# Cosine-similarity attention on one core: loads in pair order, and new orders on all engines

## The chip, the core and the metric

The kernel runs on one core of a Trainium2 chip. A core has five engines with a queue each, and each queue is worked off in the order in which the program wrote it: TensorE (PE: matmuls, and PEld, its weight loads), VectorE (DVE), ScalarE (ACT), GpSimd (POOL) and SyncE (SP, which here only issues DMAs). An instruction that waits for a semaphore holds everything behind it on its engine. The metric is the device time in microseconds; the median of the runs is compared.

## The reference

Attention on normalised vectors, for batch 8, 12 heads, 512 positions, dimension 64, in float32 (shapes are read from the inputs):

```python
Q_norm = Q / (np.linalg.norm(Q, axis=-1, keepdims=True) + 1e-10)
K_norm = K / (np.linalg.norm(K, axis=-1, keepdims=True) + 1e-10)
scores = np.einsum('bhqd,bhkd->bhqk', Q_norm, K_norm) / tau
weights = np.exp(scores - np.max(scores, axis=-1, keepdims=True))
weights = weights / (np.sum(weights, axis=-1, keepdims=True) + 1e-10)
return np.einsum('bhqk,bhkd->bhqd', weights, V)
```

With tau = 0.1 a score is at most 10 in size, so the kernel takes the exponential without subtracting the maximum.

## The kernel before

The 96 heads are worked as 48 pairs of heads, 0 to 47. Each step of a pair is one "operation" with a key, and the text names it by that key; s is the pair, w is 0 for Q and 1 for K, h the head in the pair, c one of four chunks of 128 keys.

- LD(s,w), LV(s): loads of Q, K and V of the pair, 256 KB each, issued by SyncE (lines 289 and 292; pair 0 in halves, line 286, K of pair 0 by ScalarE). ST(s): the store of the result (line 483).
- SQ(s): squares of Q and K together, on GpSimd (line 313, tile `sq`); for pairs 1 and 2 split over VectorE, ScalarE and GpSimd.
- RED(s,w): sums of the squares, on VectorE, either directly (line 341) or after TensorE has added part of them by SSQ(s,w) (lines 330 and 337).
- NEW(g,k): the reciprocal square root, for a group g of one or two pairs, in eight or nine small steps on VectorE (lines 362 to 371). For the first groups ScalarE does it instead: LOG(g), a logarithm, and NEW(g,7), an exponential (lines 355, 357; for pair 0 LOG and NRMS, lines 236, 240).
- SCL(s,w): Q or K times it (line 389): Q on VectorE, K on GpSimd for most pairs, on VectorE for ten of them.
- TR(s,w): transposes on TensorE (line 395); EVA(s): their copy out of PSUM on VectorE (line 402, tile `qt`).
- SCO(s,c): scores, two matmuls (line 429), into one of two halves of a score buffer; EXP(s,c): their exponential on ScalarE (line 445), 128x1024.
- VC(s): V to bf16 on GpSimd (line 450, tile `vb`). PV(s,h,i): weights times V on TensorE (line 459), with a column of ones that gives the sums. RCP and NRM(s,h): division on VectorE (lines 474, 476, tile `ob`).

`RINGS` sets how many buffers there are: 18 for Q and K, 6 for V, 6 for the squares, 3 each for the scaled and transposed values and the exponentials, 8 for the result. So LD(s) waits for SQ and SCL of pair s - 18, LV(s) for VC(s - 6), NRM(s) for ST(s - 8). While TensorE has nothing to do at the start, filler matmuls on zeros (`dummy`, line 188) stand in its queue.

The order of the operations on each engine is not worked out when the kernel is built. `schedule()` reads it from the constant `ORDER`: for each engine a list of numbers, each the place of an operation in the order in which the program adds it; a negative number is a filler of so many columns. `run()` then gives each operation its semaphore waits:

```python
order[e] = [self.list[int(x)] if x[0] != "-" else self.dummy(int(x[1:])) for x in text.split()]
```

Of the kernel before, what the change touches and what calls it, by code (L numbers as in the profile page):

```python
# [520 lines left out]
def slack(s, most):  # L521
# [5 lines left out]
        "7 8 64 65 103 104 143 142 224 223 11 180 181 257 105 66 258 144 182 377 334 299 300 376 333 225 259 378 453 "  # L527
        "410 487 562 335 563 301 452 411 529 715 605 412 486 528 222 987 944 945 681 639 179 564 63 606 716 791 682 454 "
        "640 102 530 141 488 911 868 758 757 607 1174 1064 1021 986 835 869 834 375 1098 332 256 836 717 451 792 298 "
        "409 641 910 683 1216 1063 1173 1139 759 793 1368 946 1402 1140 870 1020 561 638 527 912 680 1175 485 1097 1478 "  # L530
        "1444 1099 1141 988 1250 1479 604 1555 1326 1404 1215 1293 1522 1403 1249 1292 1521 1022 1065 1328 714 1674 790 "
        "1217 1369 1370 1251 867 756 1750 909 1445 985 1480 943 1749 1294 1556 1327 833 1631 1599 1632 1557 1783 1446 "
        "1825 1784 1708 1827 1709 1598 1096 1597 1062 1826 1138 1675 1673 1633 1172 1019 1523 1785 1751 1291 1214 1367 "
        "1707 1477 1248 1443 1325 1596 1401 1520 1748 1706 1630 1782 1554 1672 1824 1859 1860 "
    ),
    "pool": (
        "0 2 1 4 14 27 22 35 107 145 226 50 183 89 260 166 128 209 232 302 379 336 243 396 274 285 308 319 362 413 455 "
        "351 489 531 565 427 438 461 608 684 642 503 514 472 537 760 625 580 591 548 718 837 871 656 743 690 794 667 "
        "947 732 701 766 913 854 972 989 809 777 896 820 1066 930 1023 885 919 1201 1159 1100 1176 961 1430 995 1006 "
        "1125 1142 1218 1038 1083 1049 1354 1295 1371 1278 1114 1148 1235 1252 1507 1405 1190 1312 1388 1329 1224 1481 "  # L540
        "1267 1583 1617 1464 1447 1558 1846 1343 1524 1377 1600 1676 1419 1453 1693 1541 1811 1735 1634 1496 1769 1659 "
        "1752 1786 1710 1828 1572 1606 1648 1682 1724 1758 1800 1834 "
    ),
    "dve": (
        "5 13 15 26 28 19 67 24 21 32 70 72 37 34 75 109 78 111 76 80 114 117 149 147 115 227 119 152 155 153 184 186 "
        "229 61 187 62 188 55 189 190 56 191 157 192 263 100 194 193 101 195 196 198 94 230 95 200 303 261 305 139 133 "
        "264 140 265 134 266 234 267 380 268 171 269 271 172 270 177 339 272 337 382 178 276 340 306 341 214 342 220 "
        "343 221 344 310 345 215 346 347 254 349 255 414 348 248 416 249 385 456 353 383 458 290 417 291 418 296 419 "
        "297 420 421 490 422 387 424 423 492 324 425 325 330 532 566 429 459 367 534 368 493 331 494 609 495 463 496 "
        "373 497 374 498 401 568 499 500 685 402 407 501 408 643 505 535 611 443 569 444 570 449 571 572 450 573 574 "  # L550
        "539 575 576 612 578 477 483 645 478 577 484 582 761 614 687 519 646 520 647 525 648 526 649 719 650 616 721 "
        "651 553 653 652 554 559 654 688 560 838 658 763 596 722 597 723 602 724 603 725 795 726 727 692 729 728 636 "
        "872 630 730 797 631 637 764 734 840 672 798 673 799 948 800 678 801 914 802 768 803 679 805 804 874 807 706 "
        "806 707 712 841 990 713 811 916 748 875 749 876 843 877 878 754 879 755 880 882 881 845 883 782 783 788 950 "
        "789 1067 917 887 992 1024 951 825 952 953 826 831 954 955 956 958 957 832 921 1026 859 959 860 865 1177 866 "
        "1101 963 1069 901 1027 993 1028 907 1029 902 1030 908 1031 997 1032 1143 1033 1034 941 1036 935 1035 1103 936 "
        "1219 942 1070 1040 1145 1072 977 1104 1105 978 1106 1107 983 1108 984 1109 1296 1110 1111 1011 1179 1074 1012 "
        "1017 1112 1146 1372 1018 1116 1221 1180 1054 1181 1182 1183 1055 1184 1253 1060 1185 1061 1187 1186 1150 1188 "
        "1088 1222 1089 1094 1255 1095 1192 1406 1298 1130 1256 1131 1257 1258 1330 1259 1136 1260 1137 1261 1263 1262 "
        "1226 1265 1264 1482 1164 1332 1165 1170 1269 1171 1301 1374 1333 1206 1334 1299 1335 1212 1336 1207 1337 1338 "  # L560
        "1340 1213 1303 1339 1408 1240 1341 1246 1241 1247 1448 1375 1345 1450 1283 1409 1284 1410 1411 1289 1412 1290 "
        "1413 1414 1559 1416 1415 1417 1379 1317 1484 1323 1525 1318 1324 1451 1421 1527 1359 1485 1486 1487 1365 1488 "
        "1366 1489 1360 1490 1492 1491 1493 1455 1494 1399 1528 1393 1400 1394 1561 1601 1498 1530 1435 1603 1436 1562 "
        "1441 1563 1677 1564 1442 1565 1566 1635 1567 1532 1569 1568 1475 1711 1469 1470 1637 1476 1570 1512 1679 1513 "
        "1638 1574 1639 1640 1518 1641 1604 1642 1519 1643 1644 1645 1829 1608 1646 1552 1713 1546 1553 1547 1680 1650 "
        "1753 1755 1588 1714 1715 1716 1589 1717 1594 1718 1595 1719 1721 1720 1684 1722 1622 1789 1756 1623 1628 1726 "
        "1629 1787 1831 1664 1790 1791 1665 1792 1670 1793 1671 1794 1795 1796 1760 1832 1797 1704 1705 1698 1699 1798 "
        "1746 1747 1802 1740 1741 1836 1780 1774 1781 1775 1816 1817 1822 1823 1851 1852 1857 1858 "
    ),
    "pe": (  # L570
        "6 -256 -256 -256 20 23 -128 69 -256 -256 36 71 -128 42 33 38 108 39 43 110 46 79 77 48 148 81 146 83 118 116 "
        "85 51 52 57 58 87 53 54 59 120 185 60 228 122 154 156 124 96 97 98 99 126 262 90 158 91 92 160 135 93 136 137 "
        "162 138 197 199 164 129 130 131 132 201 304 233 203 205 231 173 174 207 167 168 169 175 170 235 176 338 237 "
        "210 211 212 213 239 381 275 273 241 216 217 218 219 277 309 279 307 281 250 251 252 253 283 244 245 246 247 "
        "311 350 415 292 313 293 315 286 287 294 352 317 288 295 289 457 354 386 384 356 320 321 322 358 323 491 360 "
        "326 327 328 329 388 390 426 428 392 363 364 365 366 394 533 430 462 460 432 397 398 399 369 400 434 370 371 "
        "372 436 567 464 403 404 405 406 466 439 440 468 441 502 504 470 442 445 610 506 446 447 448 508 538 536 510 "
        "473 474 475 479 476 512 644 480 481 540 482 542 579 581 544 515 516 517 521 546 518 686 522 523 583 524 615 "
        "585 613 549 550 551 587 552 720 555 589 556 557 558 617 619 592 593 594 655 621 595 657 762 623 598 599 600 "
        "601 659 689 661 626 627 632 628 691 663 633 634 635 665 629 796 693 695 731 733 668 697 669 670 671 839 699 "  # L580
        "674 675 676 735 767 677 765 737 702 703 704 739 705 873 741 708 709 710 769 711 808 771 744 745 746 747 810 "
        "773 915 775 750 751 752 842 812 753 814 844 778 779 816 780 784 781 785 818 949 786 787 846 884 848 821 822 "
        "823 886 824 850 991 827 828 852 920 829 888 830 918 890 855 856 857 858 892 1025 861 894 862 863 864 922 960 "
        "924 962 897 898 926 899 900 1068 928 903 904 905 906 996 964 994 966 931 932 937 938 968 933 939 940 934 970 "
        "1102 998 1037 1000 973 1039 974 975 1002 976 1144 979 980 1004 1041 1073 981 982 1043 1007 1008 1009 1045 1010 "
        "1178 1071 1047 1013 1014 1015 1016 1075 1077 1050 1115 1113 1079 1051 1052 1053 1220 1081 1147 1117 1056 1057 "
        "1149 1058 1059 1119 1084 1085 1086 1121 1087 1090 1091 1123 1092 1254 1151 1189 1093 1191 1153 1126 1127 1128 "
        "1155 1129 1297 1157 1132 1133 1223 1134 1193 1135 1195 1160 1161 1225 1197 1162 1166 1163 1199 1167 1331 1168 "
        "1169 1227 1268 1266 1229 1202 1203 1204 1205 1231 1373 1208 1233 1209 1302 1210 1211 1270 1272 1236 1237 1238 "
# [57 lines left out]
```

## Time and profile before

| | us |
|---|---|
| median of 6 runs | 193.68 |
| lowest and highest run | 191.94, 196.25 |
| the profiled execution, its time | 193.16 |
| the profiled execution, its span | 191.3 |
| ScalarE busy | 182.4 (95%) |
| TensorE, VectorE, GpSimd busy | 173.7, 168.3, 154.1 |
| first score exponential starts | 9.38 |
| last one ends | 187.98 |

Rows of the profile give, for groups of instructions, the line, the engine, what is written and read, the count, and after the bar the busy time and the mean length of one; then the idle time of the engine just before them and what ended it. In a timeline each row has start and length in us, and, in square brackets, the idle time of the engine before it and its releaser. A releaser is inferred; where it had long been done, another thing was waited for. Rows with "xN" merge N like instructions that follow each other. Consecutive instructions on one engine overlap a little in the records[...].

All of the 50.1 MB of loads and stores but 0.3 MB go through SyncE's queue (q1). The DMA engines are busy in nearly every slice up to 140 us, at 300 to 380 GB/s, and lightly after.

### The profile page before, as it was taken

How to read it: one execution, taken by the hardware profiler on the slowest of the kernel's cores; microseconds unless marked ns; L12 is line 12 of the kernel's file. 1: busy time of each engine (PE TensorE's matmuls, PEld its weight loads, DVE VectorE, ACT ScalarE, POOL GpSimd, SP SyncE). 2: the span in 40 equal slices, each digit the busy share in tenths (PEclk: the TensorE clock that was granted, in tenths of full speed). 3: DMA queues.
4: the chain of work that ended last, by engine and by line, in shares of the span. 5: the costliest groups of instructions: out<-in, count | busy, mean ns of one | idle time of the engine just before them, and what ended most of it. 6: DMA issues, size and time to landing. Idle time of an engine off the chain costs nothing.

```text
span 191.3 us, 6738 instructions
## 1 busy us (share of the span) xinstructions
PE 173.7 (91%) x2727; PEld 109.0 (57%) x2727; DVE 168.3 (88%) x588; ACT 182.4 (95%) x212; POOL 154.1 (81%) x143
## 2 busy tenths in 40 slices
PE   7799999988999898999999999999999989997973
PEld 2545655555666565656555656566655556564642
DVE  2689999989999889999999999999989989899533
ACT  4599999989999999999999999999999999999993
POOL 5399997999999799999999999999999984033000
PEclk9999999999999999999999999999999999999999
DMA  6999999999989999999999997799918033050083
GB/s 173 333 350 349 348 349 349 297 301 379 379 238 307 381 377 341 320 362 289 350 352 344 341 362 252 202 329 320 374 50 276 2 107 115 3 170 0 24 283 135
DMA packets 52302, 50.76 MB, mean 265 GB/s; under 512 B 3120, under 2 KB 52272, under 8 KB 52272
## 3 DMA queue, kind: packets, MB, share of 16 engines
q1 hardware_dynamic: 51984, 50.08, 80.4%
q8 instruction: 21, 0.34, 0.7%
q10 hardware_dynamic: 288, 0.26, 0.4%
q14 instruction: 9, 0.07, 0.1%
HBM read 37.75 MB, written 12.58 MB: 263 GB/s over the span
## 4 chain that ended last, share of the span: by engine, by line
ACT 58%; POOL 16%; DVE 8%; DMA 8%; SPq 3%; issue 3%; PE 2%; POOLq 0%
ACT et L445 58%; POOL sq L313 11%; DMA vf<-in_V_dram 4%; DMA qk<-in_Q_dram 3%; SPq L289 3%; POOL qn L389 2%; POOL vb L450 2%; DVE ob L476 2%; DVE qt L402 2%; DVE qn L389 2%; DVE nps L341 1%; PE ops L459 1%; PE scps L429 1%; PE tps L395 1%; DVE rd L474 1%
## 5 line engine op out<-in xcount | busy, mean ns | idle before, releaser
L445 ACT ACTIVATE et<-scps 128x1024 bf16<-128x1024 f32 (+1 forms) x195 | 177.4, 1105 | 1.0 <-PE scps L429 1.0
L313 POOL TENSOR_TENSOR sq<-qk 128x1024 bf16<-128x1024 f32 x45 | 84.7, 1898 | 2.0 <-DVE ob L476 1.2
L429 PE MATMUL scps<-qt 64*128 64x512 bf16 x384 | 75.5, 386 | 9.9 <-ACT et L445 6.4
L459 PE MATMUL ops<-vb,et 128*128 128x65 bf16 x1536 | 73.0, 194 | 0.4 <-DVE ob L476 0.3
L459 PEld LDWEIGHTS ops<-vb,et 128*128 128x128 bf16 x1536 | 56.0, 98 | 27.0 <-issue 17.0
L389 POOL TENSOR_TENSOR qn<-qk,rk 128x512 bf16<-128x512 f32 x37 | 38.5, 1048 | 14.2 <-DVE rk L367 8.9
L476 DVE TENSOR_TENSOR ob<-ops,rd 128x256 f32<-128x256 f32 x96 | 39.4, 415 | 1.0 <-DMA out_dram<-ob 0.6
L389 DVE TENSOR_TENSOR qn<-qk,nps 128x512 bf16<-128x512 f32 x57 | 37.9, 672 | 0.1
L395 PE MATMUL tps<-ident,qn 128*128 128x128 bf16 x376 | 33.9, 220 | 1.9 <-POOL qn L389 1.1
L429 PEld LDWEIGHTS scps<-qt 64*128 64x128 bf16 x384 | 19.0, 92 | 28.9 <-ACT et L445 12.7
L402 DVE COPY qt<-tps 128x1024 bf16<-128x1024 bf16 x47 | 32.1, 683 | 3.0 <-PE tps L395 2.8
L341 DVE TENSOR_REDUCE nps<-sq 128x8 f32<-128x512 bf16 x44 | 29.8, 682 | 1.5 <-POOL sq L313 1.5
L450 POOL TENSOR_SCALAR vb<-vf 128x512 bf16<-128x512 f32 x48 | 29.5, 632 | 1.5 <-DMA vf<-in_V_dram 1.0
L395 PEld LDWEIGHTS tps<-ident,qn 128*128 128x128 bf16 x376 | 21.6, 98 | 11.9 <-issue 3.2
L474 DVE RECIPROCAL rd<-ops 128x4 f32<-128x4 f32 x96 | 16.4, 173 | 7.1 <-PE ops L459 5.2
L330 PE MATMUL ops<-sq,ident 128*128 128x64 bf16 x400 | 20.0, 194 | 1.0 <-DVE sq L308 1.0
L330 PEld LDWEIGHTS ops<-sq,ident 128*128 128x128 bf16 x400 | 14.8, 98 | 7.0 <-issue 4.8
L337 DVE TENSOR_REDUCE nps<-ops 128x8 f32<-128x64 f32 x44 | 9.6, 220 | 1.8 <-PE ops L330 1.4
L363 DVE SCALAR_TENSOR_TENSOR nps<-nps,ys 128x32 f32<-128x32 f32 x44 | 8.5, 194 | 0.4
L362 DVE TENSOR_TENSOR nps<-nps,ys 128x32 f32<-128x32 f32 x44 | 8.4, 192 | 0.2
L367 DVE SCALAR_TENSOR_TENSOR nps<-nps,ys 128x16 f32<-128x16 f32 x29 | 5.0, 173 | 0.1
L185 PE MATMUL ops<-warm_in,ident 128*128 128x512 bf16 x8 | 3.6, 628 | 1.4 <-POOL ident L175 1.4
(43 smaller groups left out, 36.9 us busy)
## 6 DMA issues: line engine op xcount, KB each, us to landing
vf<-in_V_dram SPq DMA_DIRECT2D x48, 256.0 KB, 5.9
qk<-in_Q_dram SPq DMA_DIRECT2D x47, 256.0 KB, 6.3
qk<-in_K_dram SPq DMA_DIRECT2D x47, 256.0 KB, 5.8
out_dram<-ob SPq DMA_DIRECT2D x47, 256.0 KB, 4.7
qk<-in_Q_dram SPq DMA_DIRECT2D x2, 128.0 KB, 2.5
qk<-in_K_dram ACTq DMA_DIRECT2D x2, 128.0 KB, 2.7
out_dram<-ob SPq DMA_DIRECT2D x2, 128.0 KB, 1.7
```

Source lines behind the costliest of these rows:

```text
L313: lambda e: e.tensor_tensor(out=sqf, in0=data, in1=data, op=ALU.mult))
L330: last = e.matmul(out=o_ps[bank][:, 320:384], lhsT=ident[:, :], rhs=sq[iqs][:, 8 * w : 8 * w + 8, 8 * k : 8 * k + 8], start=(k == 0), stop ...
L341: lambda e, w=w, dst=dst: e.tensor_reduce(out=dst, in_=sq[iqs][:, 8 * w : 8 * w + 8, :], axis=AX.X, op=ALU.add))
L389: lambda e, w=w, r=r: e.tensor_tensor(out=qn[iqn][:, w].rearrange("p t h d -> p h t d"), in0=qk[iq][:, w].rearrange("p h (t d) -> p h t d" ...
L395: last = e.transpose(t_ps[:, w, t, :], qn[iqn][:, w, t].rearrange("p h d -> p (h d)"), ident[:, :])
L402: lambda e: e.tensor_copy(out=qt[iqt][:, :, :, :].rearrange("p w t x -> p (w t x)"), in_=t_ps[:, :, :, :].rearrange("p w t x -> p (w t x)")))
L429: last = e.matmul(out=sc_ps[:, 2 * b + h, :], lhsT=qt[iqt][64 * h : 64 * h + 64, 1, c, :], rhs=qt[iqt][64 * h : 64 * h + 64, 0, :, :], sta ...
L445: lambda e, c=c, b=b, hs=hs: e.activation(out=et[iet][:, c, hs[0] : hs[-1] + 1, :], in_=sc_ps[:, 2 * b + hs[0] : 2 * b + hs[-1] + 1, :], f ...
L450: lambda e: e.tensor_scalar(out=vb[:, iq, :, :, 0:DIM].rearrange("p c h d -> p h c d"), in0=vf[iv][:, :, :].rearrange("p h (c d) -> p h c ...
L459: last = e.matmul(out=o_ps[h][:, 65 * t : 65 * t + 65], lhsT=et[iet][:, c, h, 128 * t : 128 * t + 128], rhs=vb[:, iq, c, h, :], start=(c = ...
L474: lambda e, h=h, grid=grid: e.reciprocal(out=rd[io][:, h, :], in_=grid[:, :, DIM]))
L476: lambda e, h=h, grid=grid: e.tensor_tensor(out=ob[io][:, h], in0=grid[:, :, 0:DIM], in1=rd[io][:, h, :].unsqueeze(2).to_broadcast([128, N ...
```

## The change

Only the lists in `ORDER` change. The operations, their buffers and the waits of each on its data are the same; three fillers are added on TensorE. Written out in keys, the beginning of each list that moves (Q3 is LD(3,0), K3 is LD(3,1), V0 is LV(0)):

```
SyncE before   Q1 K1 Q2 K2 K3 Q3 K5 Q5 V0 Q4 K4 Q6 V2 V1 K6 V3 V4 K9 K8 Q7 K7 Q9 Q8 V5 V6 V9 K11 Q10
               K12 Q14 V8 K14 V7 ... ST2 V12 K23 Q22 K19 Q19 V15 K30 K27 K26 Q25 K21 K22 Q21 ST8 ...
SyncE after    Q1 K1 Q2 K2 V0 Q3 K3 V1 Q4 K4 V2 Q5 K5 V3 Q6 K6 V4 Q7 K7 V5 Q8 K8 V6 Q9 K9 V7 Q10 K10 V8
               Q11 K11 ST0 V9 ST1 V10 ST2 V11 ST3 ST4 Q12 K12 Q13 K13 Q14 K14 V12 Q15 K15 V13 Q16 K16 ST5
               V14 Q17 K17 ST6 V15 Q18 K18 ST7 V16 ... (one pair, one store, one V) ... Q47 K47 ST36 ...
GpSimd before  SQ2 SQ3 SQ5 VC0 SQ4 VC1 SQ6 VC3 VC2 VC4 SCL5 SQ7 SQ9 SQ8 VC5 VC9 SCL6 VC6 SCL7 VC7 VC8 SQ10
               SQ11 SCL8 SQ12 SQ13 SQ14 SCL10 VC10 SCL11 SQ15 SQ17 SQ16 SCL12 VC12 VC11 SCL13 SQ19 VC15
               SCL14 VC14 VC13 SQ18 SQ21 SQ22 SCL16 VC18 SCL17 SQ20 VC16 SQ24 SCL18 ...
GpSimd after   SQ2 VC0 SQ3 VC1 SQ4 SQ5 VC2 SQ6 VC4 VC3 SQ7 SCL5 SQ8 SQ9 VC5 SCL6 VC6 SCL7 VC7 SQ10 VC9 VC10
               SCL8 SQ11 VC8 VC11 SQ12 SQ13 SCL10 SCL11 SQ14 SQ15 SQ16 SCL12 VC14 VC12 SCL13 SQ17 SQ18 SCL14
               VC13 SQ19 SQ20 SQ21 SCL16 VC15 SCL17 VC16 SQ22 SQ23 VC17 SCL18 ...
ScalarE before LOG2 EXP(0,2) NEW(2,7) EXP(0,3) EXP(1,0) LOG3 EXP(1,1) NEW(3,7) EXP(1,2) ...
ScalarE after  LOG2 NEW(2,7) EXP(0,2) EXP(0,3) EXP(1,0) LOG3 NEW(3,7) EXP(1,1) EXP(1,2) ...
TensorE before warm, fillers 3x256, TR(0,0,0) TR(0,1,0), filler 128, SSQ(1,0), fillers 2x256, TR(0,1,1)
               SSQ(1,1), filler 128, SCO(0,1,0) ...
TensorE after  warm, fillers 5x256 192, TR(0,1,0) TR(0,0,0) SSQ(1,0), filler 192, TR(0,1,1), fillers 256 128,
               SSQ(1,1), filler 128, SCO(0,1,0) ...
VectorE before ... EVA1 NEW(2,6) SCL(2,1) RED(3,1) RED(3,0) SCL(2,0) RED(5,0) EVA2 ...
               ... NEW(6,3) NRM(4,1) NEW(6,4) EVA7 NEW(6,5) NRM(4,0) ...
VectorE after  ... NEW(2,6) EVA1 SCL(2,1) SCL(2,0) RED(3,0) RED(3,1) NEW(3,6) EVA2 ...
               ... NRM(4,0) NEW(6,2) RCP(4,1) NEW(6,3) NRM(4,1) NEW(6,4) EVA7 ...
```

In all of SyncE's new list Q, K of a pair come in the order of the pairs, and V and the stores in the order of theirs. On the other engines the lists differ in most places by a few positions: the scores keep their order on TensorE, the exponentials theirs on ScalarE. The diff, cut:

```diff
 ORDER = {
     "sp": (
-        "7 8 64 65 103 104 143 142 224 223 11 180 181 257 105 66 258 144 182 377 334 299 300 376 333 225 259 378 453 "
...
+        "7 8 64 65 103 104 11 142 143 66 180 181 105 223 224 144 257 258 182 299 300 225 333 334 259 376 377 301 410 "
...
     "pool": (
-        "0 2 1 4 14 27 22 35 107 145 226 50 183 89 260 166 128 209 232 302 379 336 243 396 274 285 308 319 362 413 455 "
...
+        "0 1 2 4 14 27 22 35 107 50 145 89 183 226 128 260 209 166 302 232 336 379 243 274 285 308 319 413 396 438 351 "
...
     "act": (
-        "9 10 3 12 25 16 17 18 29 30 31 68 106 73 44 74 40 41 45 112 47 113 49 82 150 84 151 86 88 121 123 125 127 159 "
+        "9 10 3 12 25 16 18 17 29 31 30 68 106 73 44 74 40 41 45 112 113 47 49 82 150 151 84 86 88 121 123 125 127 159 "
```

## The prediction

> **What bounds the kernel now.** I read the busy shares first, then ScalarE's timeline, then the chain back to what releases each late exponential, then GpSimd's and SyncE's timelines.
>
> ```profile
> PE 173.7 (91%) x2727; PEld 109.0 (57%) x2727; DVE 168.3 (88%) x588; ACT 182.4 (95%) x212; POOL 154.1 (81%) x143
> ```
>
> ScalarE is the bound: 182.4 of 191.3 us. Its timeline (start, duration) shows the rest:
>
> ```profile
> 4.51 0.30 ACT L236 ACTIVATE ys<-xs,eps 128x8 f32<-128x8 f32 x1 [0.22 <-DVE xs L233]
> 4.84 0.18 ACT L240 ACTIVATE scps<-ys 128x4 f32<-128x4 f32 x1
> ...
> 15.82 23.01 ACT L445 ACTIVATE et<-scps 128x1024 bf16<-128x1024 f32 x25
> 39.52 36.08 ACT L445 ACTIVATE et<-scps 128x1024 bf16<-128x1024 f32 x39 [0.70 <-PE scps L429]
> 75.87 112.11 ACT L445 ACTIVATE et<-scps 128x1024 bf16<-128x1024 f32 x123 [0.26 <-PE scps L429]
> ```
>
> After 9.38 us ScalarE stops visibly twice, at 39.52 (pair 7, chunk 3) and at 75.87 (pair 17, chunk 2). Consecutive exponentials overlap, so I count from end to end. The first one after a stop lasts 1.02 us in the same timeline, so the last row's first ends at 76.89, its second at 77.92 (the two take 2.05 us there), and the row at 187.98. From 77.92 on there are 119 full exponentials and two halves (0.49 us each): (187.98 - 77.92 - 0.98) / 119 = 0.917 us each. Against that pitch: 38.83 to 40.54 holds one exponential, 0.80 us lost; 40.54 to 75.60 holds 38, 0.21 lost; 75.60 to 76.89 holds one, 0.37 lost; 76.89 to 77.92 one, 0.11 lost. That is 1.5 us. Before 38.83 (24 in 21.99 us) and after 77.92 nothing is lost.
>
> GpSimd's and SyncE's timelines tell why:
>
> ```profile
> 32.53 1.22 POOL L450 TENSOR_SCALAR vb<-vf 128x512 bf16<-128x512 f32 x2 [0.98 <-DMA vf<-in_V_dram]
> 33.96 3.75 POOL L313 TENSOR_TENSOR sq<-qk 128x1024 bf16<-128x1024 f32 x2 [0.22 <-DMA qk<-in_K_dram]
> 37.66 1.04 POOL L389 TENSOR_TENSOR qn<-qk,rk 128x512 bf16<-128x512 f32 x1
> ...
> 63.29 3.75 POOL L313 TENSOR_TENSOR sq<-qk 128x1024 bf16<-128x1024 f32 x2 [1.20 <-DVE ob L476]
> ...
> 69.58 1.90 POOL L313 TENSOR_TENSOR sq<-qk 128x1024 bf16<-128x1024 f32 x1
> ```
> ```profile
> 49.16 0.62 SPq L292 DMA_DIRECT2D vf<-in_V_dram  x1
> 53.45 1.39 SPq L289 DMA_DIRECT2D qk<-in_K_dram  x3
> 54.88 0.47 SPq L289 DMA_DIRECT2D qk<-in_Q_dram  x1
> 55.41 0.97 SPq L289 DMA_DIRECT2D qk<-in_K_dram  x2
> 56.42 0.47 SPq L289 DMA_DIRECT2D qk<-in_Q_dram  x1
> ```
>
> First case: the 0.98 us is VC(7) waiting for V of pair 7, which SyncE issued at 23.91, behind V of pair 9, itself held for VC(3). GpSimd is full from there, so SCL(8,1) starts at 37.66; TensorE waits 0.85 us for it at the transposes of pair 8 (38.76), and the scores (7,3) stand behind those in its queue. Second case: the 1.20 us is SQ(21). Its releaser is named DVE, but that normalising multiply belongs to another pair; the load of Q of pair 21 is the 56.42 row. It was behind K of pair 30, for which SyncE stood still from 49.8 to 53.45, until pair 12 gave the buffer back. Hence SQ(20) ends at 71.5, VectorE waits 0.84 us for it in RED(20,0), SCL(18,0) comes at 73.96, TensorE waits 0.46 us at the transposes of pair 18 (74.67), and scores (17,2) are behind them. Both losses begin with a load that is issued out of its turn.
>
> **The change, part by part.** No instruction is added but three filler matmuls; the rest are moves. The sum starts from the profiled execution, 193.16 us (span 191.3, 1.86 outside it), 0.5 below the median 193.68.
>
> *Loads in pair order.* V(7) now stands behind the loads of pair 9 and waits only for VC(1); Q(21) stands behind ST(9), nine pairs ahead of K(30). Both waits above go, and with them the 1.5 us. A rule of the skill speaks against this: "SBUF — State Buffer", section "The DMA setup-cost knee", prices a transfer at about 2 us plus bytes over 436 GB/s, an estimate of 2.6 us for 256 KB. By it Q(21), issued at 56.42, lands at 59.0, before GpSimd asks at 62.1, and pair order gains nothing there. The trace's row is the one I use:
>
> ```profile
> qk<-in_Q_dram SPq DMA_DIRECT2D x47, 256.0 KB, 6.3
> ```
>
> With 6.3 us it lands at 62.7, near the 63.29 seen (longest Q or K load 8.7, shortest 2.4). The transfers are queued (about 349 GB/s from 5 to 33 us), so issue order is landing order.
>
> *GpSimd's order.* SQ(18) and SQ(20) move ahead by 4 and 7 us of work, SCL(8,1) ahead of SQ(11). From the rows, SQ takes 1.855 us, VC 0.585, SCL 1.01 (start to start). If SQ(3) starts at 11.5 (below), then 8 SQ + 9 VC + 3 SCL end and SCL(8,1) starts at 34.6, against 37.66 before. SQ(12) starts at 38.7 and SCL(12,1) at 50.0. On a clean clock chunk 0 of pair 12 is due at 38.72 + 17 x 0.917 = 54.3: lead 4.3. Before, SCL(12,1) started at 52.37 for a chunk due at 55.1, lead 2.75, and nothing was lost; so about 1.5 us of cover is left. VC steps come later in places (VC(36) by 36 us of work), but VC(36) at about 130 is for PV(36) near 145: nothing. What is late next is that same SCL(12,1), and SCL(22,1) with about as much lead.
>
> *Order of V(0).* It goes from eleventh to seventh on SyncE; Q(3) stays eighth, and K(3), which was seventh, becomes ninth. Q(3) landed at 10.72 and released GpSimd at 10.79; one more load at 349 GB/s is 0.75 us, so SQ(3) starts at about 11.5. VC(0) fills 0.6 of that. Cost by itself nothing, but ScalarE's LOG(3) hangs on SQ(3): SQ(3) ends at 13.4, its sums on TensorE at 14.0, and on VectorE RED(3,1) is now behind both SCL(2): copy of qt at 12.46, then 0.61 + 0.60 + 0.60 + 0.37, so 14.65. LOG(3) is reached at about 14.85. Cover 0.2 us; between 0 and, if K(3) takes the longest 8.7 us instead of 6.5, 2 us. I take 0.1, since the median load is near 6.5.
>
> *ScalarE's order.* The exponential that stood between LOG(2) and its own exponential, and the one behind LOG(3), move behind. The pair is now back to back and waits for its own semaphore. The head's rows show that form: 4.51 to 4.84, 0.33 us, while LOG(2) followed by a score exponential takes 0.20 (11.56 to 11.76). 0.12 us each, on the bound engine: +0.25. Two NRMS exponentials also swap, which gives VectorE its scale 0.12 us later; its copies stand behind SQ(1,0), which waits for Q(1) until 7.04: nothing.
>
> *TensorE and VectorE.* 640 more filler columns; two 256-column fillers take 0.21 us (8.04 to 8.25), so 0.27 us. 704 more go in front of the first transposes of pair 0, which feed copies that come at 7.65 anyway (cover about 0.5 us); 64 more stand between SSQ(1,0) and SSQ(1,1), 128 fewer in front. Uncovered it would be 0.27. Transposes sit on average a fraction of a chunk later before their scores, PV of head 1 later behind them; for pair 18 the lead falls from two chunks to one, as it was for pairs 4, 6 and 12 without loss. Bounds: -0.1 to +0.8 (the size of the largest loss seen); I take 0, because that lead of one chunk cost nothing where it was seen. The last PVs: four groups of head 1 now stand behind the last group of head 0, 16 x 0.04 us after data that ends 0.5 us earlier: 0 to 0.15, take 0.05.
>
> *Stores* wait in the same queue, ahead of loads. ST(4) is ahead of both loads of pair 12: rival 3.
>
> Sum: 193.16 - 1.5 + 0.25 + 0.1 + 0.05 = 192.06; I forecast 192.0.
>
> **Rivals.** *1, the wait only moves* (0.15). VectorE is 98% busy from 20 to 30 us and GpSimd without a gap; the 0.4 us by which GpSimd is behind at SQ(6), or RED(5,1) now after SQ(5) at 17.9 instead of 14.5, stops a transposition of pair 4 or 5, and the loss comes back: 193.2 to 193.7. For: TR(4) has one chunk of lead. Against: the two waits have named causes that go. *2, more than the seen loss goes* (0.17). The fastest of the runs before was 191.94, so the start-up varies by a few tenths; with LOG(3) in time and loads landing early, 191.66 less 0.3: 191.3. Against: nothing in the exponentials' pitch is left to win. *3, slower* (0.06): ST(4) holds LD(12). NRM(4,1) moves ahead of EVA(7), to about 33.3; K(12) is then issued at 34.2, and with landing time L SQ(12) starts at 34.2 + L. GpSimd is there at 38.7 with 1.5 us of cover, so the loss is L - 6.0. At the median 5.8 to 6.3 it is about nothing; over L = 7.7 the kernel is slower than its median; at 8.7 it is 194.8. For: every later load stands behind it. Against: by then 36 loads and four stores (10.5 MB) have gone through by about 33 us at 349 GB/s, so the queue is near empty and L nearer to 3.
>
> **How the numbers follow.** Likeliest case 0.62 at 192.0 (own range 191.6 to 192.6); rivals 0.17, 0.15, 0.06. Low end 191.3 from rival 2, high end 193.6 from rival 1; this leaves out rival 3 and the edges. A measurement of this kernel tells about 1% from no change: the runs before spread over 191.94 to 196.25. Faster by over 1% is below 191.74: rival 2 and a sixth of the likeliest case, 0.27. Slower by over 1% is above 195.6, the far end of rival 3 and what I have not thought of, 0.04.
>
> **What would show it.** In the profile after: ScalarE's row from 15.8 on unbroken, or broken by under 0.2 us; GpSimd without waits for loads between 12 and 150 us; SCL(8,1) near 34.6 and SQ(20) near 60; the LOG(2) to exponential distance 0.33; SQ(12) not waiting after ST(4). It is wrong if ScalarE shows a stop before 16 us (K(3)), or one near 40 to 55 us (K(12)), or if the median stays above 193 with an unbroken row, which would mean that the spread lies outside the stops.

## The result, and the profile after

The changed kernel takes 192.17 us (median of 28 runs, 191.27 to 193.00), the kernel before 193.55 us (median of 65 runs on the same chips, 191.94 to 199.38). The ratio is 0.9939, 95% interval 0.9921 to 0.9957: 0.6% faster, little, but clear of the noise. The medians of all runs are 1.4 us apart. The ratio leaves out the slow runs of the kernel before, those over 1.5% above its fastest; among the others the fastest are 0.7 us apart and the slowest 1.6 (194.56 against 193.00), so the change narrows the spread.

The page of the changed kernel's profile (granted clock in 40 slices; shares of the chain that ended last; DMA issues with the time to landing):

```profile
PEclk9889999999999999999999999999999999999999
...
ACT 91%; DMA 3%; PE 2%; DVE 1%; SPq 0%; ACTq 0%; issue 0%
...
qk<-in_Q_dram SPq DMA_DIRECT2D x47, 256.0 KB, 4.4
qk<-in_K_dram SPq DMA_DIRECT2D x47, 256.0 KB, 5.4
```

The loads of Q land 4.4 us after their issue (the median) where it was 6.3. The chain that ended last is now 91% ScalarE (58% before, with 16% GpSimd): once the exponentials run, nothing else is on it. ScalarE's timeline, the kernel changed:

```profile
10.39 0.31 ACT L355 ACTIVATE ys<-xs,eps 128x16 f32<-128x16 f32 x1 [0.83 <-DVE xs L337]
10.78 0.60 ACT L445 ACTIVATE et<-scps 128x512 bf16<-128x512 f32 x1
...
16.98 171.56 ACT L445 ACTIVATE et<-scps 128x1024 bf16<-128x1024 f32 x188
```

One row of 188 exponentials, from 16.98 to the last at 188.54: the stops at 39.5 and 75.9 are gone. Without the overlap of the first, (188.54 - 18.00 - 0.98) / 185 = 0.917 us each, the pitch of the kernel before without loss. The loss is nil.

This profiled execution took 193.87 us (span 191.8), 1.7 more than the median; it is not one of the 28. The excess lies ahead of the row: the first exponential starts at 10.78, not 9.38, and the granted clock is lower in slices 2 and 3 (more on this in the last section). A second profile of the changed kernel, experiment 8, has 191.60 us (span 189.6), the clock at 9 in every slice, the first exponential at 8.93 and the same row.

### The profile page after: what moved, and what is told of

Its sections match the earlier page's. It is cut to its first block, busy times and chain, and to the rows that moved or that the text cites. A ratio compares the mean times of both kernels' runs of the same rounds, so it can differ in the third digit from the quotient of the medians.

```text
span 191.8 us, 6749 instructions
## 1 busy us (share of the span) xinstructions
PE 176.8 (92%) x2730; PEld 111.2 (58%) x2730; DVE 169.0 (88%) x588; ACT 182.1 (95%) x212; POOL 154.5 (81%) x143
## 4 chain that ended last, share of the span: by engine, by line
ACT 91%; DMA 3%; PE 2%; DVE 1%; SPq 0%; ACTq 0%; issue 0%
ACT et L445 91%; DMA qk<-in_Q_dram 3%; PE ops L330 1%; PE scps L429 1%; DVE ob L476 0%; SPq L286 0%; DVE sq L308 0%; PE scps L188 0%; PE tps L254 0%; ACTq L85 0%; ACT xs L357 0%; PE scps L254 0%; ACT ys L355 0%; DVE rd L474 0%; PE ops L459 0%
## 5 line engine op out<-in xcount | busy, mean ns | idle before, releaser
L459 PE MATMUL ops<-vb,et 128*128 128x65 bf16 x1536 | 76.5, 194 | 0.2 <-ACT et L445 0.2
L459 PEld LDWEIGHTS ops<-vb,et 128*128 128x128 bf16 x1536 | 57.6, 98 | 29.6 <-issue 21.0
L429 PEld LDWEIGHTS scps<-qt 64*128 64x128 bf16 x384 | 19.6, 92 | 27.3 <-ACT et L445 10.3
L450 POOL TENSOR_SCALAR vb<-vf 128x512 bf16<-128x512 f32 x48 | 30.1, 637 | 1.9 <-DMA vf<-in_V_dram 1.4
L330 PEld LDWEIGHTS ops<-sq,ident 128*128 128x128 bf16 x400 | 15.3, 99 | 4.3 <-issue 2.2
```

Source lines behind the costliest of these rows:

```text
L330: last = e.matmul(out=o_ps[bank][:, 320:384], lhsT=ident[:, :], rhs=sq[iqs][:, 8 * w : 8 * w + 8, 8 * k : 8 * k + 8], start=(k == 0), stop ...
L429: last = e.matmul(out=sc_ps[:, 2 * b + h, :], lhsT=qt[iqt][64 * h : 64 * h + 64, 1, c, :], rhs=qt[iqt][64 * h : 64 * h + 64, 0, :, :], sta ...
L450: lambda e: e.tensor_scalar(out=vb[:, iq, :, :, 0:DIM].rearrange("p c h d -> p h c d"), in0=vf[iv][:, :, :].rearrange("p h (c d) -> p h c ...
L459: last = e.matmul(out=o_ps[h][:, 65 * t : 65 * t + 65], lhsT=et[iet][:, c, h, 128 * t : 128 * t + 128], rhs=vb[:, iq, c, h, :], start=(c = ...
```

## The experiments

Ranges in brackets are 95% intervals of the ratio to the kernel before, run on the same chip. "Lost" is what ScalarE's exponentials from (1,2) to (47,2) take over 0.917 us each, from end to end. Lists are written in keys, as in the section on the change.

### 1. SyncE's and GpSimd's new lists alone (e1_sp_pool)

```diff
-SyncE, GpSimd: lists of the kernel before
+SyncE, GpSimd: lists of the changed kernel
 VectorE, TensorE, ScalarE: lists of the kernel before
```

> The new lists of SyncE and GpSimd, the old ones of VectorE, TensorE and ScalarE. Theory A (the gain is the two late loads and GpSimd's place in the queue): the stops at 39.5 and 75.9 go, about 1.4 us off the kernel before, 0.2 more than the changed kernel's gain may be, since ScalarE's old order is kept: about 192.0. Rival B (the slack in VectorE's and TensorE's new lists carries the gain): at most a third of it, above 193.1, with stops left in ScalarE's row.

Measured: 210.99 us, ratio 1.0901 (1.0847 to 1.0955); lost 17.1 us. Every theory missed it. GpSimd's waits for the reciprocal root (in total, times, longest), and then one case on GpSimd and on VectorE:

```profile
POOL qn L389 <- DVE rk L367: 24.8, 11, 6.6
```
```profile
56.77 1.04 POOL L389 TENSOR_TENSOR qn<-qk,rk 128x512 bf16<-128x512 f32 x1 [3.10 <-DVE rk L367]
```
```profile
61.87 0.69 DVE L341 TENSOR_REDUCE nps<-sq 128x8 f32<-128x512 bf16 x1 [5.18 <-POOL sq L313]
```

GpSimd waits for VectorE's reciprocal root until 56.69. Two scalings and two V come next, and only then, at 59.95, the squares, for which VectorE has stood still since 56.69: each engine waits for the other in turn. So the lists go together, and a part of the gain can't be read off a part of the lists. If one follows the waits through all mixtures of whole old and new lists, only these run to the end: the kernel before, the new lists of SyncE and GpSimd together, and the new lists of SyncE, GpSimd, VectorE and TensorE together, each with either list of ScalarE. Every other mixture, SyncE's new list with GpSimd's old one among them, closes a circle of waits.

### 2. The changed kernel with ScalarE's old list (e2_act_before)

```diff
-ScalarE: LOG2 NEW(2,7) EXP(0,2) EXP(0,3) EXP(1,0) LOG3 NEW(3,7) EXP(1,1) ...
+ScalarE: LOG2 EXP(0,2) NEW(2,7) EXP(0,3) EXP(1,0) LOG3 EXP(1,1) NEW(3,7) ...
```

> The changed kernel with ScalarE's old list. Theory A: the two logarithms are followed by a score exponential again and take 0.20 instead of 0.33 us, so 0.25 us faster than the changed kernel (191.9). Rival: the distance costs nothing because the first scores come late anyway: the same 192.2.

Measured: 192.81 us, ratio 0.9976 (0.9952 to 1.0000): not the 0.25 us gain of an undone cost, rather a little slower than the change as a whole. Lost 0.72. VectorE's timeline and ScalarE's:

```profile
16.29 0.18 DVE L360 COPY nps<-xs 128x16 f32<-128x16 f32 x1 [1.39 <-ACT xs L357]
```
```profile
21.40 166.20 ACT L445 ACTIVATE et<-scps 128x1024 bf16<-128x1024 f32 x182 [0.58 <-PE scps L429]
```

In the new list of VectorE, NEW(3,6), the copy of what NEW(3,7) gives, stands ahead of EVA(2). An exponential between LOG(3) and NEW(3,7) makes VectorE wait 1.39 us there, EVA(2) with it, and five exponentials later ScalarE stops. The back-to-back order is the price of that place.

### 3 and 4. The two loads that the prediction named (e3_two_loads, e4_v7)

```diff
 SyncE of the kernel before (4: the first line alone)
-... V5 V6 V9 K11 ... Q8 V7 ...        V15 K30 K27 K26 Q25 K21 K22 Q21 ...
+... V5 V6 V7 V9 K11 ...               (unchanged in 4)
+                                      V15 Q21 K30 K27 K26 Q25 K21 K22 ...
```

> The kernel before with two loads moved and nothing else: V of pair 7 ahead of V of pair 9, Q of pair 21 ahead of K of pair 30. Theory A: GpSimd's waits at 32.5 (0.98) and 63.3 (1.20) go, ScalarE's row is whole from 15.8 on, 192.0 to 192.2. Rival B: the next late thing takes over at once, 193.2 or more. Rival C (the gain is not two named loads but the spread of landing times over all loads): the profile is whole in one execution, yet the median falls by less than half, 193.

> The kernel before with only V of pair 7 moved ahead of V of pair 9. Theory A: the stop at 39.5 (0.80 and what follows, 1.0 us) goes, the one at 75.9 (0.48) stays or grows, because GpSimd waits longer for Q of pair 21: 192.6 to 192.9. Rival B: no change, 193.5.

Measured: both loads 193.11 us, ratio 0.9975 (0.9947 to 1.0003); V(7) alone 193.59 us, 1.0008 (0.9978 to 1.0037). GpSimd's and ScalarE's timelines with both moved:

```profile
33.18 3.74 POOL L313 TENSOR_TENSOR sq<-qk 128x1024 bf16<-128x1024 f32 x2 [0.90 <-PE scps L429]
36.88 1.04 POOL L389 TENSOR_TENSOR qn<-qk,rk 128x512 bf16<-128x512 f32 x1
```
```profile
38.74 148.11 ACT L445 ACTIVATE et<-scps 128x1024 bf16<-128x1024 f32 x162 [0.52 <-PE scps L429]
```

The wait for V(7) is gone, and GpSimd waits 0.90 us at SQ(10) instead, whose K load is late next (the row names TensorE, but K(10) landed at 33.11 and SQ(10) starts at 33.18). SCL(8,1) still stands behind SQ(10) and SQ(11), starts at 36.88, and the stop at 39 stays: 0.74 lost there. In 4, V(7) alone moved (profiled execution 195.06 us, 3.6 lost), it is the same: SCL(8,1) at 37.33, a stop of 0.59 us at 39.19. So the stop of pair 7 doesn't hang on V(7) alone. The stop at 75.9 shows in neither 3 nor 4, though in 4 Q(21) was not moved. At most part of the gain is in these two loads.

### 5. SyncE's list of the kernel before, remade by need (e5_need_order)

```diff
 all other lists: kernel before
-SyncE: ... V6 V9 K11 Q10 K12 Q14 V8 K14 V7 Q11 K10 K13 Q18 Q15 V10 Q12 Q13 ST4 K25 ...
+SyncE: ... V6 Q10 V7 K10 Q11 K11 V9 V8 ST0 Q12 K12 Q13 ST1 K13 Q14 K14 ST2 V10 Q15 K15 ...
```

> The kernel before with SyncE's list alone made anew: each load in the turn in which GpSimd's old list asks for it, as soon as its buffer is free; all other lists old. Theory A2 (the order of all loads carries the gain, the two named ones were only this execution's): GpSimd hardly waits for loads, the slow executions go, median 192.0 to 192.5 with highest under 194. Rival D (the new lists of GpSimd, VectorE and TensorE carry it, by slack): 193.0 or more, with the stop near 39 still there, as SCL(8,1) stands behind SQ(11).

Measured: 200.87 us, ratio 1.0371 (1.0317 to 1.0424), lost 9.7. No theory had that. One line of GpSimd's timeline:

```profile
96.84 0.63 POOL L450 TENSOR_SCALAR vb<-vf 128x512 bf16<-128x512 f32 x1 [4.79 <-DMA vf<-in_V_dram]
```

GpSimd waits 10.5 us in four places for V. They are V of pairs 9, 24, 29 and 32. In this list V stands behind stores, and SyncE stands still for 58 us at stores and 12 at V (summed from the gaps of its timeline), with everything behind them. But the changed kernel's SyncE stands still for 73 us at stores and loses nothing, so the standing by itself is not the cost; what is lost depends on which loads stand behind, and that isn't worked out here.

### 6. The changed kernel, LOG and NEW apart, VectorE arranged for it (e6_act_dve)

```diff
 ScalarE: list of the kernel before
-VectorE: ... NEW(2,6) EVA1 SCL(2,1) ...  NEW(3,6) EVA2 ...
+VectorE: ... EVA1 NEW(2,6) SCL(2,1) ...  EVA2 NEW(3,6) ...
```

> The changed kernel with ScalarE's old list, and on VectorE the copies EVA(1) and EVA(2) ahead of NEW(2,6) and NEW(3,6), as they were. If the loss with ScalarE's old list alone came from VectorE waiting for NEW(2,7) and NEW(3,7) with the copies behind, it goes here, and the 0.25 us that the back-to-back exponentials cost come off: 191.9. Rival (the first 16 us are set by landings, so neither matters): 192.2 to 192.4, like the changed kernel.

Measured: 191.94 us, ratio 0.9896 (0.9865 to 0.9927); the changed kernel on the same chip 191.63 us, 0.9890 (0.9826 to 0.9954). No gain (the changed kernel has four runs there). From the first score exponential to the end of EXP(1,2) ScalarE takes 7.47 us in the kernel before, 7.74 in the changed one (experiment 8) and 7.86 here. So the price of back-to-back, 0.27 us, is there, and undoing it exposes another wait: LOG(3) starts at 14.21, when the sums of SQ(3) are ready, and waits for them.

### 7. The changed kernel, each V from pair 6 on two pairs later (e7_v_late2)

```diff
-SyncE: ... Q8 K8 V6 Q9 K9 V7 Q10 K10 V8 Q11 K11 ST0 V9 ST1 V10 ST2 V11 ST3 ST4 Q12 K12 Q13 K13 Q14 K14 V12 ...
+SyncE: ... Q8 K8 Q9 K9 Q10 K10 V6 Q11 K11 ST0 V7 ST1 V8 ST2 V9 ST3 ST4 Q12 K12 Q13 K13 Q14 K14 V10 ...
```

> The changed kernel with each V from pair 6 on issued two pairs later (in the place of V two pairs on). Theory A2: GpSimd waits for V again, ScalarE's row breaks in several places from 40 us on: 193 to 196. Rival D: the slack of the new lists takes it up, 192.2 to 192.5.

Measured: 241.56 us, ratio 1.2436 (1.2306 to 1.2566), lost 48.6: slower, as the theory of V's place had it, but by far more. SyncE's timeline, then GpSimd's:

```profile
31.76 2.48 SPq L483 DMA_DIRECT2D out_dram<-ob  x2
34.28 0.47 SPq L289 DMA_DIRECT2D qk<-in_Q_dram  x1
...
37.38 0.47 SPq L292 DMA_DIRECT2D vf<-in_V_dram  x1
```
```profile
42.73 0.63 POOL L450 TENSOR_SCALAR vb<-vf 128x512 bf16<-128x512 f32 x1 [8.73 <-DMA vf<-in_V_dram]
```

V(10) is the row at 37.38: behind ST(3), ST(4), which wait for their pairs until 34.2, and behind six loads of Q and K. It lands 5.3 us later, GpSimd has stood at VC(10) for 8.73 us, and SCL(8,1) behind it. ScalarE's next exponential waits 8.35 us, so ST(5) is issued at 49.60 only, and the V behind it still later. It feeds on itself: 51 us of waits for V in 13 places.

### 8. The changed kernel again (e8_changed_again)

> The changed kernel once more, for a second profile: if the late first exponential of its profiled execution (10.78 against 9.38 us) belongs to that execution, it is near 9.4 here and the span near 190.3; if it belongs to the new filler list, it is above 10 again with the granted clock of TensorE below 0.9 in the first 10 us. ScalarE's row whole from 16 us on in both cases; median 192.2.

Measured: 191.63 us (four runs, 191.60 to 191.64), ratio 0.9890 (0.9826 to 0.9954). ScalarE's timeline:

```profile
8.93 0.58 ACT L445 ACTIVATE et<-scps 128x512 bf16<-128x512 f32 x1
...
11.11 0.31 ACT L355 ACTIVATE ys<-xs,eps 128x16 f32<-128x16 f32 x1
11.45 0.22 ACT L357 ACTIVATE xs<-ys 128x16 f32<-128x16 f32 x1
...
14.75 171.56 ACT L445 ACTIVATE et<-scps 128x1024 bf16<-128x1024 f32 x188
```

GpSimd's:

```profile
35.07 1.04 POOL L389 TENSOR_TENSOR qn<-qk,rk 128x512 bf16<-128x512 f32 x1 [0.41 <-DVE nps L367]
...
39.10 3.74 POOL L313 TENSOR_TENSOR sq<-qk 128x1024 bf16<-128x1024 f32 x2
...
92.46 1.89 POOL L313 TENSOR_TENSOR sq<-qk 128x1024 bf16<-128x1024 f32 x1 [0.50 <-DMA qk<-in_K_dram]
...
127.34 1.89 POOL L313 TENSOR_TENSOR sq<-qk 128x1024 bf16<-128x1024 f32 x1 [0.86 <-DMA qk<-in_K_dram]
```

And SyncE's, at K(12), behind ST(3), ST(4) and Q(12):

```profile
34.87 0.49 SPq L289 DMA_DIRECT2D qk<-in_K_dram  x1
```

ScalarE's row is whole, and yet GpSimd waits 4.5 us for loads from 12 us on, against 3.0 in the profile before (the 1.2 at SQ(21), whose releaser is named VectorE, included). But the waits lie elsewhere. Between 24 and 125 us, where all stops of the first profile before are, GpSimd waits 2.3 to 4.4 us for loads in the kernel before and its load orders (before, 3, 4, 10, 12; the longest wait 0.9 to 1.4; counted by the landings, since the names are inferred). In the five profiles with the new lists on SyncE, GpSimd, VectorE and TensorE (after, 2, 6, 8, 11) it waits 0.3 to 0.8 us, 0.5 the longest; V(7) and Q(21) are in time in all five. Their waits after 125 us are longer, 3.7 us here. So in the stretch where loads were late before, they are now in time.

### 9. As 5, with the stores later (e9_need_stores_late)

```diff
-SyncE (5): ... Q11 K11 V9 V8 ST0 Q12 K12 Q13 ST1 K13 Q14 K14 ST2 V10 Q15 K15 ...
+SyncE (9): ... Q11 K11 Q12 V9 V8 K12 Q13 K13 Q14 K14 V10 Q15 K15 ST0 Q17 K17 Q16 K16 V12 ST1 ...
```

> As the list by need, but each store put where its pair has been divided for some 8 us in the profiled execution of before, so that SyncE should not stand at a store with loads behind it. All other lists old. Theory S (a V load behind a store that SyncE stands at is what costs; the order of loads by itself is worth the 1.4 us): 192.0 to 192.6. Rival D (the gain needs the new lists of GpSimd, VectorE and TensorE): 193.0 to 194.0, with SyncE and GpSimd hardly waiting for one another, and ScalarE's stop near 39 still there.

Measured: 199.68 us, ratio 1.0324 (1.0264 to 1.0385), lost 8.35. It decides nothing. GpSimd waits 8.8 us for V in four places (longest 4.0), SyncE stands 23 us at V for a buffer and 44 at stores. Fewer waits at stores, more at V: which of the two holds the loads isn't told apart.

### 10. The kernel before again (e10_before_again)

> The kernel before, for a second profile. Theory C (its stops move from one execution to the next with the landings): ScalarE's row breaks again near 39, and at other places than 75.9, with GpSimd waiting for other loads than V of pair 7 and Q of pair 21. Rival: the same two stops at the same places, 0.9 and 0.5 us.

Measured: 197.90 and 195.52 us, slower than 43 and 40 of the 43 other runs of the kernel before on this chip (191.40 to 196.60). The profiled execution (197.90) on ScalarE, then on GpSimd:

```profile
58.34 45.02 ACT L445 ACTIVATE et<-scps 128x1024 bf16<-128x1024 f32 x49 [0.76 <-PE scps L429]
103.90 5.61 ACT L445 ACTIVATE et<-scps 128x1024 bf16<-128x1024 f32 x6 [0.54 <-PE scps L429]
110.02 82.81 ACT L445 ACTIVATE et<-scps 128x1024 bf16<-128x1024 f32 x91 [0.52 <-PE scps L429]
```
```profile
101.45 0.62 POOL L450 TENSOR_SCALAR vb<-vf 128x512 bf16<-128x512 f32 x1 [1.27 <-DMA vf<-in_V_dram]
```

The same program stops at 57, 58, 104 and 110 us, and neither at 39 nor at 76. Lost 2.7 us against 1.5 in the first profile. But it is not a second sample of the same conditions. The clock is low at its start (last section), and EXP(1,2) ends 3.6 us later than in the first profile, while V(7) lands at 31.74, earlier than the 32.45 there: GpSimd asks for it at 35.08 only, so it is in time, and the stop of pair 7 is gone. That stop is there in the three profiles that start in time, with SCL(8,1) behind both squares and the stores where they were (before, 3, 4). The stops at 104 and 110, pair 24 chunk 0 and pair 25 chunk 2, come again in 4 and in 12. So the places are not drawn anew each time: the kernel before has a few weak places, and which of them open depends on the execution. That this also holds between two executions that both start in time is not shown.

### 11. Experiment 6 with the sums of SQ(3) earlier (e11_first16)

```diff
-SyncE: ... K2 V0 Q3 K3 V1 Q4 ...       GpSimd: SQ2 VC0 SQ3 VC1 ...   VectorE: ... SCL(2,0) RED(3,0) RED(3,1) EVA2 ...
+SyncE: ... K2 Q3 K3 V0 V1 Q4 ...       GpSimd: SQ2 SQ3 VC0 VC1 ...   VectorE: ... RED(3,0) RED(3,1) SCL(2,0) EVA2 ...
```

> The changed kernel with ScalarE's old list, EVA(1) and EVA(2) ahead of NEW(2,6) and NEW(3,6), and further V of pair 0 behind K of pair 3 on SyncE, SQ(3) ahead of VC(0) on GpSimd, RED(3,0) and RED(3,1) ahead of SCL(2,0) on VectorE. If LOG(3) waits for SQ(3), and that ate what ScalarE's old list gives back, SQ(3) starts 0.7 us earlier and 0.25 to 0.4 us come off the changed kernel: ratio to before 0.985 to 0.992 where the changed kernel has 0.989 to 0.994. Rival (something else holds the first scores): no difference from the changed kernel.

Measured: 192.07 us, ratio 0.9938 (0.9914 to 0.9961): no better than the changed kernel. LOG(3) no longer waits, but GpSimd does at 18.79 (1.22 us, for a load), and ScalarE stops at 20.33 (0.23) and 21.51 (0.16). The wait has moved by some five microseconds. No version tried beats the changed kernel clearly.

### 12. The kernel before, both seen stops taken away at their roots (e12_loads_scl8)

```diff
-SyncE: ... V5 V6 V9 K11 Q10 K12 ... V7 Q11 K10 ...   Q21 ahead of K30, as in 3     GpSimd: ... SQ10 SQ11 SCL8 ...
+SyncE: ... V5 V6 V7 Q10 K10 V9 K11 K12 ...                                          GpSimd: ... SQ10 SCL8 SQ11 ...
```

> The kernel before with five moves: V of pair 7, Q and K of pair 10 ahead of V of pair 9, Q of pair 21 ahead of K of pair 30, and SCL(8,1) ahead of SQ(11) on GpSimd. My first theory, completed (the two seen stops are the loss): no stop at 39 or 76, 192.0. Rival C (most of the loss of the median lies in stops that change from run to run): the profile is nearly whole, yet the median is 192.9 or more, and the highest runs stay above 195.

Measured: 193.72 us, ratio 1.0000 (0.9965 to 1.0036). ScalarE's timeline:

```profile
60.00 38.79 ACT L445 ACTIVATE et<-scps 128x1024 bf16<-128x1024 f32 x42 [0.16 <-PE scps L429]
99.27 5.61 ACT L445 ACTIVATE et<-scps 128x1024 bf16<-128x1024 f32 x6 [0.47 <-PE scps L429]
105.39 83.67 ACT L445 ACTIVATE et<-scps 128x1024 bf16<-128x1024 f32 x91 [0.52 <-PE scps L429]
```

The stops at 39 and 76 are gone, as wanted, and the kernel loses 3.1 us, at 60, 99, 105 and in smaller pieces. Nothing gained in 22 runs. The stops at 99 and 105 have one root. SyncE's, GpSimd's and TensorE's timelines:

```profile
89.97 0.43 SPq L292 DMA_DIRECT2D vf<-in_V_dram  x1
```
```profile
96.82 0.62 POOL L450 TENSOR_SCALAR vb<-vf 128x512 bf16<-128x512 f32 x1 [1.35 <-DMA vf<-in_V_dram]
97.41 1.04 POOL L389 TENSOR_TENSOR qn<-qk,rk 128x512 bf16<-128x512 f32 x1
```
```profile
98.51 0.40 PE L395 MATMUL tps<-ident,qn 128*128 128x128 bf16 x4 [0.51 <-POOL qn L389]
```

Counted off in the lists, the V is that of pair 36, and the scaling behind it is SCL(25,1). V(36) needs the buffer of V(30), which VC(30) gives back at 89.94, and it takes 6.8 us to land. GpSimd's old list asks for it 5.5 us after VC(30), just ahead of SCL(25,1): TensorE waits 0.51 us for it at the transposes of pair 25, and the scores (24,0) stand behind those. GpSimd has no gap from there to SCL(26,1), which is then late for (25,2). It is the same V(36) at 101.45 in 10. In the first profile before, V(36) landed 5.2 us after its issue, and GpSimd waited 0.05 us. So the root is GpSimd's order: it takes a V eleven pairs ahead of its turn and stands at it. In the new list VC(36) comes in its turn, at 131.80 in experiment 8, 9.9 us after V(36) has landed.

## Why the prediction was right, and where it was not

The time was right, 192.0 for 192.17, and so was the likeliest case, faster by less than 1%. The reason given for the largest term was wrong in part. The number did not suffer, since it needs only that the loss goes, and not what caused it.

**The floor: right.** It was 193.16 less 1.5 lost. The rows of both profiles of the changed kernel have nothing lost, at the same 0.917 us. What was to be won was the loss and no more; rival 2's 191.3 is the fastest run (191.27), not the median. That the profile before was of a middling execution, 0.5 us below its median, was luck: the same sum from the execution of 10, 197.90 us with 2.7 lost, would have given 195.6.

**Loads in pair order: the size right, the cause right only in part.** "Both waits above go" held: V(7) and Q(21) are in time in all five profiles with the new lists. The step that failed is "Both losses begin with a load that is issued out of its turn", and with it "and with them the 1.5 us". Moving the two loads gave 0.9975, one of them 1.0008, and taking both stops away at their roots 1.0000.

What the runs show in its place: the losses begin on GpSimd as much as on SyncE. The stop of pair 7 stays with V(7) in time, since K(10) is late in its stead and SCL(8,1) stands behind both squares (3, 4). It goes when SCL(8,1) moves ahead of a square and V(7), Q(10) and K(10) come earlier, all together (12). The stops of pairs 24 and 25 (4, 10, 12) begin with V(36), which GpSimd takes too early. The prediction looked at that move, "VC(36) by 36 us of work", asked only what it costs, and put it at nothing; that the old place could cost something was not considered. In the old list GpSimd takes V up to 15 pairs ahead of the last pair whose K it has scaled, in the new one up to 5.

"GpSimd without waits for loads between 12 and 150 us" came true between 24 and 125 us but for 0.8 us, and not after. What remains doesn't reach ScalarE: every profile with the new lists (after, 2, 6, 8, 11) is without a stop after 22 us, while each of the kernel before and its load orders (before, 3, 4, 10, 12) has one, and loses 0.9 to 3.6 us (5 and 9 lose more). An example of the same size: in 4 GpSimd waits 1.03 us at 128.64 for V(37), with two squares and V(47) still ahead of SCL(34,1), and ScalarE stops for 0.24 us at 135.38; in the changed kernel it waits 1.37 us at 130.08 for SQ(40), SCL(34,1) is next, and nothing stops. How the gain divides between loads in time, the new order on GpSimd and more slack elsewhere isn't shown: the mixtures of lists that would tell don't run (1), and a kernel before with VC(36) alone in its turn was not tried. From the start of SCL(s,1) on GpSimd to the first exponential of its pair there are at least 3.5 us in both profiles of the changed kernel and at least 2.8 in both of the kernel before; that this lead helps is argued, not shown.

**The price of a transfer: the row was the better base.** The Trainium skill, "SBUF — State Buffer", section "The DMA setup-cost knee", gave an estimate of 2.6 us; the median landing is now 4.4 to 5.4 us with the loads in order. But the stop less that the forecast made of it can't be told from chance, since the stop at 76 is in neither 4 nor 10, where Q(21) was not moved. And "issue order is landing order" holds only roughly: in the first profile before, 8 of 143 neighbours among the loads land swapped, by up to 1.3 us.

**GpSimd's times: right within 0.7 us, where the start is in time.** In experiment 8 SCL(8,1), due at 34.6, came at 35.07, after 0.41 us for VectorE; SQ(12) 38.7, came 39.10; SCL(12,1) 50.0, came 50.36; SQ(20) near 60, came at 60.7. In the other profile of the changed kernel, with its late start, each is 2.2 us later. The lead of pair 12 was put at 4.3 and is 3.55 in both, the smallest of all.

**V(0) and LOG(3): cost nothing for 0.1.** In experiment 8 SQ(3) started at 10.63 for 11.5, LOG(3) at 14.28 for 14.85, without a wait. That the cover is small is seen in 6: 0.2 us earlier on ScalarE, and LOG(3) waits.

**ScalarE's order: right, 0.27 for 0.25,** and 0.34 us from LOG(2) to its exponential for 0.33. What the prediction did not see is what the order buys: 1.39 us on VectorE (2).

**TensorE: right at nothing.** No stop at pairs 4, 5, 12 or 18; from the last exponential to the end of the span it is 3.3 us in both kernels, so the 0.05 for the last PVs is nothing too.

**Rivals.** The first, that the wait only moves, is what happens on GpSimd when V(7) alone is moved (3, 4: to K(10)), not with the whole change. The third, ST(4) ahead of the loads of pair 12, has the times it gave (K(12) issued at 34.87 for 34.2) and no cost, SQ(12) running on at 39.10. That such a place can cost much is seen in 7: with V two places further behind the same two stores the kernel takes 24% longer.

## What to carry to other kernels

When a tuned kernel stops in a few places, profile it a second time, and a few variants with it, before you name the culprits: here one stop stayed when the late load in front of it was put in time, and another weak place did not show in the first profile at all. Compare executions that start alike, since a late start alone brings loads into time. Waits of a supplier should be compared by where they lie, not by their sum. The size of the gain can still be forecast from one profile, as the bound engine's own pitch without stops. In a queue that works in order, ask of every item not only whether it is late, but whether it need stand there yet; and expect that lists made together don't work in halves.

## What the runs showed of the hardware

ScalarE's exponentials follow each other at 0.917 us from end to end, but the recorded length of one grows from 1.02 us just after a stop to a mean of 1.22 over the changed kernel's run: each starts before the recorded end of the one before. Small losses therefore leave no idle time in the timeline, like the 0.21 us between the two stops of the kernel before, and have to be counted from end to end.

The start differs between executions of one kernel by more than the change is worth. TensorE's timeline at the sums of Q(1), eight matmuls, first in the changed kernel's profile, then in that of the kernel before:

```profile
8.15 0.61 PE L330 MATMUL ops<-sq,ident 128*128 128x64 bf16 x8 [1.53 <-DVE sq L308]
```
```profile
7.79 0.41 PE L330 MATMUL ops<-sq,ident 128*128 128x64 bf16 x8 [1.01 <-DVE sq L308]
```

Q(1) landed at 7.38 in the one, at 7.04 in the other. TensorE's wait is half a microsecond longer, and then the same eight matmuls take 0.61 us instead of 0.41, and so do those after them, up to the first exponential at 10.78. Experiment 10, the kernel before, does the same: Q(1) at 7.63, a wait of 1.75 us, 0.61 us for the eight, the first exponential at 10.97, and on its page the granted clock

```profile
PEclk9756999999999999999999999999999999999999
```

In experiment 8 TensorE doesn't wait there, the clock is 9 in every slice, and the first exponential comes at 8.93. So the slow start is not made by the three new fillers. It goes with 1.4 to 2.0 us at the first exponential, and in 10 with 2.0 us more up to EXP(1,2).

The length of that one wait is not the rule: in 1 the eight take 0.61 us after a wait of 0.64, in 7 they take 0.41 after 0.68. The traces' clock records show a better one. The granted clock is 0.50 from 7.99 to 11.40 us in the changed kernel's profile, and from 7.67 to 17.91 in 10; all changes in a trace lie on a grid of 3.41 us. In the 3.41 us ahead of the fall TensorE was busy for 1.55 and 1.70 us, in the kernel before for 2.40 (6.47 to 9.88), without a fall. Over all 14 profiles, from the first record of each on, the clock fell after 25 such stretches, with TensorE busy for 61% of each at most, and stayed up after 723, with 58% at least. So less than some 60% goes with a fall; no run here sets it on purpose. The Trainium skill, "TensorE: Matmul & The Clock Gate", "Part 1: The HAM clock gate", has the clock fall after an idle window of about 3.4 us that runs freely, so that the same kernel can differ from run to run. Grid and difference are what these traces show; but the stretch need not be idle throughout.
